# A hybrid attention, state-space and expert layer: the experts' weight pieces stored as contiguous blocks in the chip's memory

## The chip, the core and the metric

The kernel runs on one core of one Trainium2 chip, the other cores idle. The metric is the device time of one execution in microseconds; the median of the runs counts. Laying out the inputs with numpy on the host happens ahead of the execution and is no part of that time.

## The reference, cut to what matters

The layer is attention and a state-space branch, a product with `w_out`, a norm, and then a mixture of experts with a second norm. The change touches the mixture alone. Of 32 experts, each token (256 of them, 2048 features) is sent to two; an expert is a gated product of three matrices, gate and up of 2048 × 512 and down of 512 × 2048, all float32:

```python
def hierarchical_moe(h, ..., w_gate, w_up, w_down):
    ...
    def expert_block(args):
        tok, e = args
        xb = h[tok]
        return (jax.nn.silu(xb @ w_gate[e]) * (xb @ w_up[e])) @ w_down[e]
```

The three matrices of all experts are 32 × 3 × 4.19 MB = 403 MB, of 472 MB that the kernel moves in all. Every expert is computed, so all of them are loaded once.

## The kernel before, in words

**Front.** Up to about 430 us the kernel computes the projections, the two mixers, `w_out`, the first norm and the routing.

**The experts** come in 16 pairs (0 to 15), 64 token places for each expert of a pair. A pair is one pass of the loop behind line 1333: gather its tokens' features (`gather`, L1165), gate and up products (L1340: each weight piece is the moving operand, 512 columns, the two experts side by side in the two halves of the array's columns), silu times up (`hidden`, L1228 and L1229), a transpose (L1233), the down products in four column chunks (L1370), and the weighted sums back to token order (`weighted`, `combine`, L1192 to L1205). While one pair's down products run, the next pair's tokens are gathered. Pairs 2 to 7 also add the residual's rows (`res_rows`, L1090; `residual`, L1102 and L1107). The last pair works in half-sized pieces, so that less is left to do behind the last load.

**The weight pieces.** The list `items` (L974 to L982) holds the loads in the order of use: per pair eight gate, eight up and eight down pieces of 1 MB, alternating between the two experts; in the last pair sixteen of each at 0.5 MB. A gate or up piece is four of the sixteen feature tiles: feature p·16 + k lies on partition p, so the piece reads 8 KB in one stretch for each partition, and partitions lie 32 KB apart. A down piece is one of four column chunks: partition p holds rows 4p to 4p + 3, and of each row 512 columns, which are four stretches of 2 KB, 8 KB apart. In the last pair gate and up pieces read 4 KB per partition, and down pieces four stretches of 1 KB.

**What sets the order of the loads.** All of them are issued by SP, in the order of `items`. `ring_load` (L988) takes a free slot of SBUF (8 KB per partition; `RING`, L56, lists 21 of them) and issues the load; `ring_take` (L1014) hands the tile to the matmuls and puts the slot back on the list; `ring_fill` (L1021) issues as many further loads as there are free slots. A load waits on SP for the last reader of its slot and for earlier loads in flight, and every load behind it in SP's order waits with it. The two places that form a load's source are these:

```python
                nc.sync.dma_start(t, src[e].rearrange("(p f) d -> p f d", p=P)[:, :, lo:lo + w])
            else:
                nc.sync.dma_start(t, src[e].rearrange("(p k) f -> p (k f)", p=P)[:, q[0] * FE:(q[0] + q[1]) * FE])
```

**Behind the pairs** a loop takes tokens past an expert's first 64 in blocks of 128 (L1389 on; the number of blocks is read at run time), with loads of its own (L1423, L1434), and then comes the second norm and the store (L1443 to L1468).

Of the kernel before, what the change touches and what calls it, by code (L numbers as in the profile page):

```python
# [17 lines left out]
PSUM = bass.MemoryType.PSUM  # L18

P = 128  # L20
T = 256
D = 2048
# [10 lines left out]
NE = 32  # L33
# [4 lines left out]
# 8 KB slots of SBUF per partition, by use  # L38
# [21 lines left out]
def bcast_rows(ap, n=P):  # L60
    """A DRAM row vector, the same on n partitions."""
    return bass.AP(tensor=ap.tensor, offset=ap.offset, ap=[[0, n]] + [list(d) for d in ap.ap])
# [3 lines left out]
def block_kernel(ctx: ExitStack, tc: tile.TileContext, I: dict, out: bass.AP):  # L66
# [23 lines left out]
    # ---------------------------------------------------------------- first loads  # L90
# [9 lines left out]
    # ---------------------------------------------------------------- constants  # L100
# [108 lines left out]
    # ---------------------------------------------------------------- the dense products' weight pieces  # L209
    # a piece: four k-tiles of a column chunk, split into two parts of 12 significant bits each  # L210
# [41 lines left out]
    # ---------------------------------------------------------------- x transposed, in two parts  # L252
# [23 lines left out]
    # ---------------------------------------------------------------- parameter columns, rotary tables  # L276
# [14 lines left out]
    def rope_table(tab, pos, n, cols, name):  # L291
        """cos and sin of position * inv_freq: [n, cols, (cos, sin), 8]."""
        pf = fr.tile([n, cols, 1], F32, name=name + "_pf")
        dve.tensor_copy(pf[:, :, 0], pos)
        ang = wk.tile([n, cols, 2, 8], F32, name=name + "_ang", tag="qrt")
        for j in range(8):
            dve.tensor_scalar(ang[:, :, :, j], pf.to_broadcast([n, cols, 2]), float(INV_FREQ[j]), None, op0=OP.mult)
        k = wk.tile([n, cols, 2, 8], F32, name=name + "_k", tag="qrs")
        dve.tensor_scalar(k[:, :, 0], ang[:, :, 0], 1.0 / (2 * math.pi), 0.25, op0=OP.mult, op1=OP.add)
        dve.tensor_scalar(k[:, :, 1], ang[:, :, 1], 1.0 / (2 * math.pi), None, op0=OP.mult)  # L300
        dve.tensor_scalar(k, k, MAGIC, None, op0=OP.add)
        dve.tensor_scalar(k, k, -MAGIC, None, op0=OP.add)
        kf = k.rearrange("p a b c -> p (a b c)")
        af = ang.rearrange("p a b c -> p (a b c)")
        for c in (TWO_PI_1, TWO_PI_2, TWO_PI_3):
            dve.scalar_tensor_tensor(af, kf, -c, af, op0=OP.mult, op1=OP.add)
        dve.tensor_scalar(ang[:, :, 0], ang[:, :, 0], math.pi / 2, None, op0=OP.add)
        dve.tensor_scalar(ang, ang, 3.1415925, -3.1415925, op0=OP.min, op1=OP.max)
        act.activation(tab, ang, AF.Sin)

    def rope(dst, src, cos, sin, tmp):
        """dst[..., 0:16] = src[..., 0:16] rotated."""
        x1, x2 = src[..., 0:8], src[..., 8:16]
        dve.tensor_mul(tmp[..., 0:8], x2, sin)
        dve.tensor_mul(tmp[..., 8:16], x1, sin)
        dve.tensor_mul(dst[..., 0:8], x1, cos)
        dve.tensor_mul(dst[..., 8:16], x2, cos)
        dve.tensor_sub(dst[..., 0:8], dst[..., 0:8], tmp[..., 0:8])
        dve.tensor_add(dst[..., 8:16], dst[..., 8:16], tmp[..., 8:16])

    # ---------------------------------------------------------------- dense products
# [59 lines left out]
    # ---------------------------------------------------------------- what follows a chunk  # L381
# [96 lines left out]
    # ---------------------------------------------------------------- gates, time steps  # L478
# [4 lines left out]
    def gates_dt():  # L483
        gf = gates.rearrange("p a h c -> p (a h c)")
        act.activation(gf, gf, AF.Exp, scale=-1.0)
        dve.tensor_scalar(gf, gf, 1.0, None, op0=OP.add)
        dve.reciprocal(gf, gf)
        # softplus = max(x, 0) + ln(1 + exp(-|x|))
        dneg = fr.tile([P, 2, 16], F32, name="dneg")
        dve.tensor_scalar(dneg, dt, -1.0, None, op0=OP.mult)  # L490
        dve.tensor_tensor(dneg, dneg, dt, op=OP.min)
        act.activation(dneg, dneg, AF.Exp)
        act.activation(dneg, dneg, AF.Ln, bias=1.0)
        dve.tensor_scalar(dt, dt, 0.0, None, op0=OP.max)
        dve.tensor_add(dt, dt, dneg)
        act.activation(nega, nega, AF.Exp)
        dve.tensor_scalar(nega, nega, -1.0, None, op0=OP.mult)
        for a in range(2):
            dve.tensor_mul(dta[:, a], dt[:, a], nega)
# [17 lines left out]
    # ---------------------------------------------------------------- compressed keys and values  # L517
# [22 lines left out]
    def cmp_hidden():  # L540
        # four column tiles: (k or v, parity of the k-tile)
# [41 lines left out]
    def cmp_keys_t():  # L583
# [4 lines left out]
        # per group: high parts, low parts  # L588
# [18 lines left out]
    # ---------------------------------------------------------------- attention  # L607
# [24 lines left out]
    def cmp_scores(g):  # L632
        """Probabilities of the compressed branch times its gate: [token, (head, block)]."""
# [87 lines left out]
    # ---------------------------------------------------------------- state space branch (one chunk, no earlier state)  # L721
# [98 lines left out]
    # ---------------------------------------------------------------- router on the sums before the first norm  # L820
    # logits = rstd * (sums @ (g * W) - mean * colsum(g * W)) + (b @ W + bias)
# [42 lines left out]
    def router_t(c):  # L864
        """Logits transposed, [36, token], from two k-tiles in two column tiles at once."""
# [20 lines left out]
    # ---------------------------------------------------------------- the order of the work  # L886
# [80 lines left out]
    # ---------------------------------------------------------------- the experts' weight pieces, in the order of use  # L967
    wgate, wup, wdown = I["w_gate"][0], I["w_up"][0], I["w_down"][0]
# [3 lines left out]
    # k-tiles of a gate or up piece  # L972
    GU = [(k, 4) for k in range(0, KT, 4)], [(k, 2) for k in range(0, KT, 2)]
    items = []  # L974
    for pr in range(NE // 2):
        gu = [(nm, src, 2 * pr + u, q) for nm, src in (("g", wgate), ("u", wup)) for q in GU[pr == LASTP] for u in range(2)]
        dn = [("d", wdown, 2 * pr + u, (lo, w)) for c, lo, w in (DOWN_LAST if pr == LASTP else DOWN) for u in range(2)]
        # the last two loads before the first pair go where the sums before the norm lie
# [5 lines left out]
    def second(i):  # L984
        """The last pair's pieces are half as large, a slot for two; the other half of a slot that is open."""
        return items[i][2] == 2 * LASTP + 1

    def ring_load(n=1):  # L988
        for i in range(ring["next"], min(ring["next"] + n, len(items))):
# [15 lines left out]
            if nm == "d":  # L1005
                lo, w = q
                t = t.rearrange("p (f d) -> p f d", f=4)
                nc.sync.dma_start(t, src[e].rearrange("(p f) d -> p f d", p=P)[:, :, lo:lo + w])
            else:
                nc.sync.dma_start(t, src[e].rearrange("(p k) f -> p (k f)", p=P)[:, q[0] * FE:(q[0] + q[1]) * FE])  # L1010
# [39 lines left out]
    # ---------------------------------------------------------------- first norm, without its scale and shift  # L1050
# [22 lines left out]
    # feature d = 16 q + k goes to [k, q]  # L1073
# [11 lines left out]
    # the residual alpha * (normed * g + b): rows over the partitions  # L1085
# [10 lines left out]
    def residual(j, a):  # L1096
        """Column chunk j of the scaled rows (j < 4), or of the shift (j >= 4), into the sums."""
# [11 lines left out]
    # ---------------------------------------------------------------- routing  # L1109
# [3 lines left out]
    # the group of the largest logit, the first of equals  # L1113
# [12 lines left out]
    # its two best experts, the first of equals  # L1126
# [20 lines left out]
    # rank among the expert's tokens, from 1; 0 where the token is not the expert's  # L1147
# [3 lines left out]
    # ---------------------------------------------------------------- experts, in pairs, 64 tokens each  # L1151
# [36 lines left out]
    def weighted(py, wsl, i):  # L1188
        """The weighted outputs of a chunk, in two parts that one pass each carries."""
# [20 lines left out]
    def sums_first(lo, w):  # L1210
        """The sums so far, to which a chunk's outputs come in PSUM."""
# [13 lines left out]
    def hidden(pg, pu, xg):  # L1225
        """silu(gate) * up, transposed; both in the second half of a tile for gathered tokens."""
# [15 lines left out]
    def weights():  # L1242
        """Softmax over the two best, times the group's probability."""
# [19 lines left out]
    # tokens past an expert's first 64 go in blocks of 128: which block is whose  # L1263
# [32 lines left out]
    # scale and shift of the second norm, over the partitions  # L1296
    gb = {}

    def split_rows2():
        """The rows in two parts, on partitions 0 and 32 up, that one pass adds up exactly."""  # L1300
# [84 lines left out]
    # ---------------------------------------------------------------- tokens past an expert's first 64  # L1385
# [3 lines left out]
    with tc.For_i(0, nblk, 1) as b:  # L1389
# [29 lines left out]
        for src, pp in ((wgate, pg), (wup, pu)):  # L1419
            for q in range(4):  # L1420
                t = slot(OVER[n % 4], "w_o")
                n += 1
                nc.sync.dma_start(t, src[bass.ds(e, 1)].rearrange("o (p q k) f -> p (o q) (k f)", p=P, q=4)[:, q])  # L1423
# [7 lines left out]
        for c in range(4):  # L1431
            t = slot(OVER[n % 4], "w_o").rearrange("p (f d) -> p f d", f=4)
            n += 1
            nc.sync.dma_start(t, wdown[bass.ds(e, 1)].rearrange("o (p f) d -> p (o f) d", p=P)[:, :, c * 512:(c + 1) * 512])  # L1434
# [6 lines left out]
    # ---------------------------------------------------------------- second norm  # L1441
# [43 lines left out]

# [15 lines left out]
```

## Time and profile before

| | |
|---|---|
| median of 3 runs | 1416.79 us (1415.51 to 1418.05) |
| span of the profiled execution, first to last instruction | 1414.3 us |
| its own time | not listed apart; the median lies 2.5 us above the span |
| TensorE matmuls busy | 1326.1 us, 94% |
| VectorE, ScalarE, GpSimd busy | 515.3 us, 358.0 us, 159.1 us |
| moved by DMA | 472.12 MB in 157686 packets, mean 334 GB/s |
| loads of gate, up and down, 1 MB each | 120 of each; 18.0, 19.8 and 14.5 us from issue to landing (median) |
| mean granted clock of TensorE | 0.983 of 2.4 GHz |

Matmuls are pipelined and their ends are modelled, so that a busy TensorE isn't one at its peak. The DMA share of a window is the mean busy share of the core's 16 DMA engines; it can read a few per cent above 1, which is to be taken as always busy. A window's row gives the stretch, its length, busy time and count of instructions of PE (TensorE matmuls), PEld (its weight loads), DVE (VectorE), ACT (ScalarE) and POOL (GpSimd), then the granted clock, the DMA share and GB/s. A timeline's row gives the start, the time taken, the engine, the line and what it writes from what.

### The profile page before, as it was taken

To read this page: it belongs to the slowest core of one execution; us is meant where nothing else is said; L and a number is where in the kernel's file an instruction comes from. 1 tells how busy PE (TensorE), PEld (TensorE's weight loads), DVE (VectorE), ACT (ScalarE), POOL (GpSimd) and SP (SyncE) were. 2 spreads that over 40 slices of the span, in tenths; PEclk is the share of its full clock that TensorE was granted. 3 is DMA by queue.
4 is the path that set the end of the run, shared out by engine and by line. 5 is a ranking of instruction groups with operands and counts; after the bars stand their busy time and mean duration, and the time that the engine had idled before them with its cause. 6 is when DMAs were issued, how large, how long until landed. Compare 5 with 4: busy or idle time off the path is not lost. (4 is left out here: it accounts for less than half of the span.)

```text
span 1414.3 us, 18310 instructions
## 1 busy us (share of the span) xinstructions
PE 1326.1 (94%) x7381; PEld 765.6 (54%) x7381; DVE 515.3 (36%) x1095; ACT 358.0 (25%) x695; POOL 159.1 (11%) x87
## 2 busy tenths in 40 slices
PE   7998999999999999999999999999999998989994
PEld 6778899997784444434444343443444344343442
DVE  6757677568842323132131221312213021121216
ACT  4544566546423211111011110211101011010122
POOL 3432233334520000000000000000000000000001
PEclk9999999999999999999999999999999999999997
DMA  8852334436998999999999999999999999999993
GB/s 286 301 170 99 120 103 137 149 127 214 315 375 311 363 374 414 407 404 417 400 420 400 413 408 404 417 399 421 401 412 409 403 418 399 420 400 411 400 373 137
DMA packets 157686, 472.12 MB, mean 334 GB/s; under 512 B 17923, under 2 KB 32383, under 8 KB 126623
## 3 DMA queue, kind: packets, MB, share of 16 engines
q1 hardware_dynamic: 157008, 470.84, 86.4%
q8 instruction: 60, 0.98, 0.3%
q14 instruction: 28, 0.22, 0.0%
q0 software_dynamic: 288, 0.08, 0.0%
q10 hardware_dynamic: 302, 0.00, 0.0%
HBM read 468.79 MB, written 2.10 MB: 333 GB/s over the span
## 5 line engine op out<-in xcount | busy, mean ns | idle before, releaser
L1370 PE MATMUL p_dn<-wd,xg 128*64 128x512 f32 (+1 forms) x1088 | 244.6, 591 | 15.4 <-DVE work L1193 14.2
L1340 PE MATMUL p_up<-wu,xg 128*64 128x512 f32 x1024 | 229.1, 593 | 9.0 <-DMA wu<-in_w_up 9.0
L1340 PE MATMUL p_gate<-wg,xg 128*64 128x512 f32 x1024 | 226.0, 597 | 0.0
L243 POOL TENSOR_TENSOR w_lo<-raw,w_hi 128x1024 fp32r<-128x1024 f32 x52 | 141.6, 2727 | 252.1 <-ACT w_hi L242 239.0
L1340 PEld LDWEIGHTS p_up<-wu,xg 128*64 128x64 f32 x1024 | 76.3, 137 | 157.7 <-issue 134.3
L1229 DVE TENSOR_TENSOR xg<-xg,p_up 128x512 f32<-128x512 f32 x16 | 11.0, 688 | 409.0 <-ACT xg L1228 409.0
L1370 PEld LDWEIGHTS p_dn<-wd,xg 128*64 128x64 f32 x1088 | 74.8, 140 | 145.2 <-issue 109.3
L1340 PEld LDWEIGHTS p_gate<-wg,xg 128*64 128x64 f32 x1024 | 71.7, 137 | 143.7 <-issue 140.4
L1193 DVE SCALAR_TENSOR_TENSOR work<-p_dn,wsl,work 128x512 fp32r<-128x512 f32 (+1 forms) x68 | 48.9, 719 | 273.5 <-ACT work L1192 273.5
L1165 PEld LDWEIGHTS p_g<-S,hp 128*128 128x128 f32 x1024 | 120.8, 194 | 28.3 <-issue 26.0
L1165 PE MATMUL p_g<-S,hp 128*128 128x128 f32 x1024 | 127.2, 281 | 0.9 <-DVE cnt L1318 0.9
L1464 POOL TENSOR_TENSOR sum<-sum,row 128x512 f32<-128x512 f32 x4 | 6.7, 1692 | 995.7 <-DVE sum L1456 995.7
L242 ACT CAST w_hi<-raw 128x1024 fp32r<-128x1024 f32 (+1 forms) x112 | 108.5, 1020 | 31.9 <-PE p_acc L367 11.5
L1192 ACT ACTIVATE work<-p_dn,wsl 128x512 fp32r<-128x512 f32 (+1 forms) x68 | 45.2, 665 | 281.9 <-PE p_dn L1370 278.8
L345 PE MATMUL p_acc<-xh,w_hi 128*128 128x256 f32 x384 | 112.5, 293 | 0.0
L1228 ACT ACTIVATE xg<-p_gate 128x512 f32<-128x512 f32 x16 | 9.6, 597 | 406.6 <-PE p_up L1340 406.6
L347 PE MATMUL p_acc<-xl,w_hi 128*128 128x256 f32 x384 | 109.6, 285 | 0.0
L348 PE MATMUL p_acc<-xh,w_lo 128*128 128x256 f32 x384 | 109.6, 285 | 0.0
L243 DVE TENSOR_TENSOR w_lo<-raw,w_hi 128x1024 fp32r<-128x1024 f32 (+1 forms) x60 | 77.5, 1292 | 28.3 <-ACT w_hi L242 28.1
L1205 DVE TENSOR_TENSOR sum<-sum,p_co 128x512 f32<-128x512 f32 (+1 forms) x130 | 79.7, 650 | 9.4 <-PE p_co L1201 9.4
L1201 PE MATMUL p_co<-work,swT 128*128 128x512 f32 (+1 forms) x268 | 76.7, 408 | 0.0
L345 PEld LDWEIGHTS p_acc<-xh,w_hi 128*128 128x128 f32 x384 | 74.8, 195 | 0.7
(401 smaller groups left out, 1482.7 us busy)
## 6 DMA issues: line engine op xcount, KB each, us to landing
wg<-in_w_gate SPq DMA_DIRECT2D x120, 1024.0 KB, 18.0
wu<-in_w_up SPq DMA_DIRECT2D x120, 1024.0 KB, 19.8
wd<-in_w_down SPq DMA_DIRECT2D x120, 1024.0 KB, 14.5
raw<-in_w_in SPq DMA_DIRECT2D x36, 1024.0 KB, 5.0
raw<-in_w_out SPq DMA_DIRECT2D x16, 1024.0 KB, 5.2
wg<-in_w_gate SPq DMA_DIRECT2D x16, 512.0 KB, 10.8
wu<-in_w_up SPq DMA_DIRECT2D x16, 512.0 KB, 10.2
wd<-in_w_down SPq DMA_DIRECT2D x16, 512.0 KB, 8.9
```

What stands on the lines that cost most here:

```text
L242: act.copy(hi[:, ks, s], raw[:, ks])
L243: eng.tensor_tensor(lo[:, ks, s], raw[:, ks], f(hi[:, ks, s]), op=OP.subtract)
L345: pe.matmul(dst, hi[:, k, s], xk(xh, kt), start=(first and k == 0 and j % 2 == 0), stop=False, skip_group_check=True)
L347: pe.matmul(dst, hi[:, k, s], xk(xl, kt), start=False, stop=False, skip_group_check=True)
L348: pe.matmul(dst, lo[:, k, s], xk(xh, kt), start=False, stop=(last and k == 3), skip_group_check=True)
L1165: pe.matmul(at(k), hpm[a][:, 4 * c + k], S[:, a], start=(a == 0), stop=(a == 1))
L1192: act.activation(hi, py, AF.Copy, scale=wsl)
L1193: dve.scalar_tensor_tensor(lo, py, wsl, f(hi), op0=OP.mult, op1=OP.subtract)
L1201: pe.matmul(pc, swT[:, a * P:(a + 1) * P], part, start=(y == 0), stop=(y == 1))
L1205: dve.tensor_add(acc[a][:, s], acc[a][:, s], pc)
L1340: pe.matmul(pp[64 * u:64 * u + 64, :], xg[:, kk, 64 * u:64 * u + 64], tl[u][:, k], start=(kk == 0), stop=(kk == KT - 1), skip_group_check= ...
L1370: pe.matmul(py[64 * u:64 * u + 64, :], aT[:, q, 64 * u:64 * u + 64], tl[u][:, q], start=(q == 0), stop=(q == 3), skip_group_check=True)
```

## The change

The host stores the experts' weights in another order before the launch. `w_gate` and `w_up` become [expert, quarter, partition, 2048 elements], `w_down` [expert, column chunk, partition, 4 rows × 512 columns]; each 1 MB piece is then one contiguous block, 8 KB per partition. For the last pair's half chunks of down there is a further array, `w_down_last`, cut in eight, 4 KB per partition; the last pair's gate and up pieces read half of a partition's 8 KB, as they read 4 KB before. What lands in SBUF, and where, stays as it was, and so does all arithmetic. The loads of the loop over tokens past 64 follow the new order. Comments and docstrings go, too, so that line numbers behind L963 move by one to fourteen.

```diff
-    wgate, wup, wdown = I["w_gate"][0], I["w_up"][0], I["w_down"][0]
+    wgate, wup, wdown, wdown_last = I["w_gate"], I["w_up"], I["w_down"], I["w_down_last"]
...
             if nm == "d":
                 lo, w = q
+                nc.sync.dma_start(t, src[e, lo // 512] if w == 512 else wdown_last[e - 2 * LASTP, lo // w])
                 t = t.rearrange("p (f d) -> p f d", f=4)
-                nc.sync.dma_start(t, src[e].rearrange("(p f) d -> p f d", p=P)[:, :, lo:lo + w])
             else:
-                nc.sync.dma_start(t, src[e].rearrange("(p k) f -> p (k f)", p=P)[:, q[0] * FE:(q[0] + q[1]) * FE])
+                nc.sync.dma_start(t, src[e, q[0] // 4][:, q[0] % 4 * FE:(q[0] % 4 + q[1]) * FE])
                 t = t.rearrange("p (k f) -> p k f", f=FE)
...
-                nc.sync.dma_start(t, src[bass.ds(e, 1)].rearrange("o (p q k) f -> p (o q) (k f)", p=P, q=4)[:, q])
+                nc.sync.dma_start(t, src[bass.ds(e, 1), q].rearrange("o p x -> p (o x)"))
...
-            nc.sync.dma_start(t, wdown[bass.ds(e, 1)].rearrange("o (p f) d -> p (o f) d", p=P)[:, :, c * 512:(c + 1) * 512])
+            nc.sync.dma_start(t, wdown[bass.ds(e, 1), c].rearrange("o p x -> p (o x)"))
+            t = t.rearrange("p (f d) -> p f d", f=4)
...
+def _laid_out(inputs):
+
+    a = {name: np.ascontiguousarray(inputs[name]) for name in _INS}
+    for name in ("w_gate", "w_up"):
+        a[name] = np.ascontiguousarray(a[name][0].reshape(NE, P, 4, 4 * FE).transpose(0, 2, 1, 3))
+    down = a["w_down"][0].reshape(NE, P, 4, D)
+    cut = lambda v, n: np.ascontiguousarray(v.reshape(len(v), P, 4, n, D // n).transpose(0, 3, 1, 2, 4)).reshape(
+        len(v), n, P, -1)
+    a["w_down"], a["w_down_last"] = cut(down, 4), cut(down[-2:], 8)
+    return a
...
-    for name in _INS:
-        a = np.ascontiguousarray(inputs[name])
+    for name, a in _laid_out(inputs).items():
```

The order of the instructions is the same on every engine. On SP, at the change from the first pair's pieces to the second's, the kernel before issues these (`wg`, `wu` and `wd` are gate, up and down pieces; the sizes are the target's partitions and elements, as the source is cut):

```order
L1010 DMA wu<-in_w_up 128x2048 x5
L1008 DMA wd<-in_w_down 128x4x512 x5
L1010 DMA wu<-in_w_up 128x2048 x2
L1008 DMA wd<-in_w_down 128x4x512 x3
L1010 DMA wg<-in_w_gate 128x2048 x8
```

and the changed kernel, at the same place:

```order
L1011 DMA wu<-in_w_up 128x2048 x5
L1008 DMA wd<-in_w_down 128x2048 x5
L1011 DMA wu<-in_w_up 128x2048 x2
L1008 DMA wd<-in_w_down 128x2048 x3
L1011 DMA wg<-in_w_gate 128x2048 x8
```

Nothing moved; a down piece's four stretches of 512 elements became one of 2048. In the last pair, 128x4x256 became 128x1024 in the same way.

## Rows read from the trace of the kernel before

**Rows 1.** The page: engines, busy tenths in 40 slices, DMA packets.

```profile
PE 1326.1 (94%) x7381; PEld 765.6 (54%) x7381; DVE 515.3 (36%) x1095; ACT 358.0 (25%) x695; POOL 159.1 (11%) x87
...
PE   7998999999999999999999999999999998989994
...
DMA  8852334436998999999999999999999999999993
...
DMA packets 157686, 472.12 MB, mean 334 GB/s; under 512 B 17923, under 2 KB 32383, under 8 KB 126623
```

**Rows 2.** The windows, cut at each pair's first gate matmul.

```profile
core 0: us, PE busy (x) PEld busy (x) DVE busy (x) ACT busy (x) POOL busy (x), PEclk, DMA share, GB/s
...
554.97:615.61 60.64, 58.10 (x286) 25.19 (x285) 15.00 (x27) 7.42 (x18) 0.00 (x0) 0.97 1.02 408
615.61:674.56 58.95, 56.40 (x286) 24.78 (x285) 15.02 (x27) 7.42 (x18) 0.00 (x0) 1.00 1.03 409
...
913.76:971.50 57.74, 55.18 (x283) 24.57 (x282) 11.61 (x23) 7.42 (x18) 0.00 (x0) 1.00 1.03 408
971.50:1029.25 57.75, 55.20 (x283) 24.58 (x282) 11.62 (x23) 7.41 (x18) 0.00 (x0) 1.00 1.02 408
1029.25:1090.90 61.65, 57.95 (x283) 25.96 (x282) 11.62 (x23) 7.42 (x18) 0.00 (x0) 0.97 1.03 409
1090.90:1152.34 61.44, 57.96 (x284) 25.39 (x283) 11.63 (x23) 7.42 (x18) 0.00 (x0) 0.97 1.02 409
1152.34:1213.00 60.66, 56.50 (x284) 24.91 (x283) 11.62 (x23) 7.42 (x18) 0.00 (x0) 1.00 1.02 408
1213.00:1274.90 61.90, 56.63 (x284) 24.82 (x283) 11.62 (x23) 7.42 (x18) 0.00 (x0) 1.00 1.02 408
1274.90:1336.47 61.57, 56.48 (x283) 25.61 (x282) 12.89 (x26) 8.03 (x19) 0.00 (x0) 1.00 1.03 405
```

**Rows 3.** TensorE's waits, 1029 to 1337 us: sum, times, longest.

```profile
PE p_up L1340 <- DMA wu<-in_w_up: 9.0, 8, 1.4
```

**Rows 4.** The timeline of the last pair's end; landing of its down loads (us).

```profile
1380.01 1.96 PE L1370 MATMUL p_dn<-wd,xg 128*64 128x256 f32 x16
...
1382.58 2.41 PE L1370 MATMUL p_dn<-wd,xg 128*64 128x256 f32 x16
...
1385.59 2.35 PE L1370 MATMUL p_dn<-wd,xg 128*64 128x256 f32 x16
...
1388.53 0.65 PE L1370 MATMUL p_dn<-wd,xg 128*64 128x256 f32 x2
1389.67 1.94 PE L1370 MATMUL p_dn<-wd,xg 128*64 128x256 f32 x14 [0.50 <-SPq L1389]
...
1380.34 1.41 SPq L1008 DMA_DIRECT2D wd<-in_w_down  x1
...
DMA to landing us min/median/max: 8.9/8.9/8.9
```

**Rows 5.** The windows by piece: gate/up, down, last gate/up, last down, x.

```profile
528.00:548.00 20.00, 17.45 (x91) 8.23 (x91) 5.62 (x12) 4.63 (x11) 0.00 (x0) 1.00 1.01 420
560.00:580.00 20.00, 20.00 (x96) 6.75 (x94) 3.42 (x5) 0.00 (x0) 0.00 (x0) 1.00 1.05 387
1340.00:1356.00 16.00, 16.00 (x77) 5.79 (x73) 0.00 (x0) 1.65 (x5) 0.00 (x0) 1.00 1.03 410
1376.00:1384.00 8.00, 8.00 (x65) 4.97 (x62) 6.31 (x17) 1.43 (x3) 0.00 (x0) 1.00 1.10 348
318.00:324.00 6.00, 6.00 (x32) 4.47 (x31) 4.31 (x9) 2.73 (x3) 3.00 (x1) 1.00 1.04 425
```

**Rows 6.** The timeline of SP's DMA queue: first gate issues of pairs 2, 10, 15.

```profile
511.20 11.11 SPq L1010 DMA_DIRECT2D wg<-in_w_gate  x8
...
1004.13 11.76 SPq L1010 DMA_DIRECT2D wg<-in_w_gate  x8
...
1312.88 22.01 SPq L1010 DMA_DIRECT2D wg<-in_w_gate  x16
```

More of the change, by code (lines that the diff above doesn't have):

```diff
@@ L1431, in block_kernel @@
         for c in range(4):
-            t = slot(OVER[n % 4], "w_o").rearrange("p (f d) -> p f d", f=4)
+            t = slot(OVER[n % 4], "w_o")
             n += 1
-            nc.sync.dma_start(t, wdown[bass.ds(e, 1)].rearrange("o (p f) d -> p (o f) d", p=P)[:, :, c * 512:(c + 1) * 512])
+            nc.sync.dma_start(t, wdown[bass.ds(e, 1), c].rearrange("o p x -> p (o x)"))
+            t = t.rearrange("p (f d) -> p f d", f=4)
             py = bank("acc", "p_dn")
```

## The prediction

> **What bounds the kernel now.** The page comes first. TensorE shows as busy in 94% of the span, and so do the DMA engines: from the eleventh of the forty slices to the last but one both lines read 9 or 8 [rows 1]. Two resources that look full can't both be the bound of one stretch, so the next view is the windows, cut at the first gate matmul of each pair of experts [rows 2]. Call the pairs 0 to 15. Pairs 8 and 9 each take 57.75 us. Pairs 2 to 7 also carry the residual rows; they take 58.95 us, or 60.64 us where the granted clock fell. Those two differ by 1.7 us, and the longer one shows a mean clock of 0.97 in place of 1.00, a short stay on the lower of the two levels (1.2 instead of 2.4 GHz). Pairs 10 to 14 do the work of 8 and 9 and take 60.66 to 61.90 us.
>
> What they wait for stands in the waits of TensorE in that stretch: only the wait on the loads of the up weights is new, 9.0 us in 8 stalls [rows 3]. That row counts idle time alone. Around each stall the matmul stream also thins out, so I price the stalls by the lengths of the pairs: 61.65 + 61.44 + 60.66 + 61.90 + 61.57 = 307.2 us against 5 × 57.75 = 288.75 us, an excess of 18.5 us. Two of the five show the clock of 0.97, so 2 × 1.7 = 3.4 us is the clock's, and **15.1 us** the loads'.
>
> The last pair stalls too [rows 4]. Sixteen of its down matmuls should take 1.96 us, and three groups take 2.41 us, 2.35 us, and 3.08 us (0.65 us, a gap, then 1.94 us, ending at 1391.61 from 1388.53): together **2.0 us** too long. The last piece was issued at 1380.34 and landed 8.9 us later, at 1389.2, and the matmuls go on right behind it.
>
> Why do the loads fall behind only after pair 9? A pair's weights are 24 pieces of 1.049 MB, 25.17 MB. In windows that hold mainly pieces of one kind, the engines all busy, gate and up move at 420 GB/s and down at 387 [rows 5]. A pair therefore costs the DMA engines 16.78/0.420 + 8.39/0.387 = 39.95 + 21.7 = 61.6 us, more than TensorE needs. The ring hides that until its lead is eaten up: SP issued pair 2's first gate load at 511.20, 43.8 us before its use, and pair 10's at 1004.13, 25.1 us before [rows 6, 2]. At 25 us the stalls begin. The usable lead is **18.7 us**.
>
> **The change, part by part.**
>
> *Down pieces of pairs 0 to 14.* Each partition now reads 8 KB in one run, not four runs of 2 KB. Rates go with the run length: 348 GB/s for 1 KB (the last pair's down), 387 for 2 KB, 410 for 4 KB (the last pair's gate and up), 420 for 8 KB [rows 5]. A sixteenth of each, per engine, gives 47, 85, 160 and 312 ns per run: an estimate of some 10 ns per run beside 37 ps per byte. This is why I take 420 for the new down pieces: their form becomes that of the gate pieces. The ends are 387 (the run length isn't the cause) and 425 (the load of x into the sums, the one transfer of a whole contiguous megabyte, 318 to 324 us [rows 5]). The pair then costs 25.17/0.420 = 59.9 us, 1.7 us less.
>
> The Trainium skill has another price for short runs, in "DMA: Bandwidth & Descriptors", section "Why small descriptors are slow (HBM only)": about 3 extra cycles per packet on top of one per 32 bytes. By that, 2 KB against 8 KB would be only 3.5% apart, an estimate of 400 GB/s for the new down pieces; the rows here show 9% between the two lengths. What a rate part of the way would give is the first rival.
>
> *Gate and up pieces.* Their runs were 8 KB before, too; only the distance from partition to partition shrinks, from 32 to 8 KB. I take zero. Above it the bound is again 425, 1%; below it no row has an 8 KB run slower than 420, and what a loss would cost is the third rival.
>
> *Last pair.* Down goes from 1 KB to 4 KB runs, 348 to 410 GB/s: 24.1 to 20.5 us. Gate and up keep 4 KB runs.
>
> *Issues, engines, the overflow loop.* The order on SP and on each engine stays. The loop over tokens past 64 isn't entered in the trace (no row on its loads), so its edits cost nothing. What SP takes to issue isn't on the path: a pair's issues run 25 us and more ahead of their use, and were that cover gone, the stalls priced above would be what it costs. The layout is made on the host ahead of the launch.
>
> **The ledger.** Where the DMA engines need less than TensorE, the ring stays full and nothing more is won, since pieces wait for slots. Pairs 2 to 7 last 358.8 us (554.97 to 913.76), 59.8 each, against 59.9: the lead falls by 0.7 us. Pairs 8 to 14 fall by 7 × (59.9 − 57.75) = 15.1 us, or 11.7 with two clock drops. Of 18.7 us, 2.9 to 6.3 remain, so **no pair stalls**. Last pair: 1389.2 − 1312.88 = 76.3 us passed from its first issue to the last landing, 65.0 of them transfer (40.9 + 24.1), 11.3 backlog. Now 61.4 + 11.3 = 72.7 us. TensorE wants that piece 51.2 us after the pair's first matmul (1388.53 − 1336.47, less the two earlier stalls), so at least 25.1 + 2.9 + 51.2 = 79.2 us after the first issue. It is there 6 us early.
>
> What is late next is TensorE itself, with the lengths of pairs 8 and 9. The gain is 15.1 + 2.0 = **17.1 us**. The profiled span, 1414.3 us, becomes 1397.2; the median of the runs lies 2.5 us above the span, which gives **1399.7 us**.
>
> The clock is the unknown left: 1.7 us per drop. Drops in pairs 1 to 9 (three here) used to be swallowed by the later wait for loads; now each counts. None in the last five pairs gives 1396.3, five 1404.8.
>
> **The rivals.**
>
> 1. *Part of the way.* The new down pieces get halfway, 403 GB/s. The pair costs 39.95 + 20.8 = 60.8 us; the lead falls by 6 × 1.0 + 7 × 3.05 − 3.4 = 24 us, 5 more than there is: 1405 us. Against it: one price per run fits all four lengths. This is what the skill's 3 cycles would come to. Chance 0.08.
>
> 2. *Nothing.* The down pieces' lower rate isn't due to the runs, or the source isn't one run after all: 387 stays, the lead is eaten as before, 1416.8 us. Against it: 1 and 4 KB runs in the last pair lie apart in the same way, with other neighbours; of 157686 packets, all but 31,000 are under 8 KB [rows 1], which is what 240 gate and up pieces of 128 runs give, so such a tile does load in 8 KB runs. The Trainium skill ("DMA: Bandwidth & Descriptors", section "Where 436 GB/s comes from") says that the memory's share of about 358 GB/s binds such loads, by which run length wouldn't matter; the 420 GB/s of this trace disagrees. Chance 0.05.
>
> 3. *Slower.* A piece is now one contiguous megabyte, and the sixteen engines read close together. If that costs rate, it hits all 24 pieces. The point that decides is the mean of now, 25.17/61.6 = 409 GB/s. At 400 a pair costs 62.9 us, 1.3 more; 14 pairs bind one after the other from the ring's filling on, 18 us, less some 2 us won in the last pair: 1433 us. For it: no row shows a long stream of such pieces. Against it: the 425 GB/s of x. Chance 0.06.
>
> **How the numbers follow.** My forecast has a chance of 0.80, the rivals 0.08, 0.05 and 0.06; 0.01 is left over. The likeliest time is 1399.7 us. The forecast's own range is 1395 to 1405: up to five drops of the clock up, and down the none of them, with 1 us for the early pairs. I let the range go to 1406, which takes in rival 1 and leaves out rivals 2 and 3, with a tail below. About 0.2%, 2.8 us, is what a measurement of this kernel tells from no change: the three runs lie 2.5 us apart. Forecast and rival 1 are faster beyond that, 0.88; rival 2 is the same, with the leftover, 0.06; rival 3 slower, 0.06.
>
> **What would show it.** Right: the windows of the down pieces move 420 GB/s; pairs 10 to 14 take 57.75 us, or 59.45 with a clock below 1.00; the wait of the up matmuls on loads is gone; first issue to use stays above 25 us; packets fall by 52,224 (136 transfers, three runs in four gone), to about 105,000. Wrong: the down windows stay under 400, or gate and up fall below 420, or stalls remain in pairs 13 to 15 although the rates are right; then the ring's lead, not the rate, was misread.

## The result, and the profile after

The changed kernel takes 1398.8 us (median of 4 runs, 1397.74 to 1399.46) against 1417.4 us for the kernel before, measured beside it (4 runs, 1415.51 to 1418.23): a ratio of 0.9868, 95% interval 0.9854 to 0.9882. The forecast was 1399.7 us.

Two lines of the page after, and its packets, answer to [rows 1]. The DMA engines are still busy to the end, and yet no matmul waits for a load any more:

```profile
PE   7998999999999999999999999999999999999994
...
DMA  8943333446897899999999999999999999999991
...
DMA packets 105461, 472.12 MB, mean 338 GB/s; under 512 B 17922, under 2 KB 24190, under 8 KB 59038
```

52,225 packets are gone. The windows cut at each pair's first gate matmul, as in [rows 2]: pairs 2 and 3, then pairs 9 to 14. Columns as there.

```profile
core 0: us, PE busy (x) PEld busy (x) DVE busy (x) ACT busy (x) POOL busy (x), PEclk, DMA share, GB/s
556.82:617.47 60.65, 58.10 (x286) 25.18 (x285) 15.00 (x27) 7.42 (x18) 0.00 (x0) 0.97 1.01 420
617.47:676.42 58.95, 56.41 (x285) 24.78 (x284) 15.03 (x27) 7.42 (x18) 0.00 (x0) 1.00 1.01 421
...
973.37:1031.12 57.75, 55.19 (x283) 24.58 (x282) 11.62 (x23) 7.42 (x18) 0.00 (x0) 1.00 1.01 421
1031.12:1088.87 57.75, 55.20 (x284) 24.60 (x283) 11.62 (x23) 7.42 (x18) 0.00 (x0) 1.00 1.01 421
1088.87:1146.62 57.75, 55.19 (x283) 24.58 (x283) 11.62 (x23) 7.42 (x18) 0.00 (x0) 1.00 1.01 421
1146.62:1204.37 57.75, 55.20 (x284) 24.59 (x283) 11.63 (x23) 7.42 (x18) 0.00 (x0) 1.00 1.01 421
1204.37:1263.75 59.38, 56.82 (x283) 24.97 (x282) 11.61 (x23) 7.42 (x18) 0.00 (x0) 0.97 1.01 421
1263.75:1321.50 57.75, 55.19 (x283) 24.59 (x283) 12.90 (x26) 8.03 (x19) 0.00 (x0) 1.00 1.02 414
```

Pairs 10 to 14, formerly 60.66 to 61.90 us, are now at the 57.75 us of pair 9, save pair 13, whose clock of 0.97 costs it 1.6 us. Their DMA rate, 405 to 409 GB/s before, is 421 now, in pair 14 414. These are all waits of TensorE's matmuls from 440 to 1400 us (sum, times, longest); the wait on a load, which stood in [rows 3] with 9.0 us, is gone:

```profile
PE p_sw L1178 <- ACT xg L1235: 24.0, 15, 1.6
PE p_dn L1371 <- DVE work L1194: 14.3, 30, 0.5
PE p_ht L1234 <- DVE xg L1230: 1.5, 1, 1.5
PE p_dn L1371 <- ACT xg L1235: 0.7, 1, 0.7
PE p_co L1215 <- DVE sum L1206: 0.3, 1, 0.3
```

The timeline of the last pair's down groups answers to [rows 4]. Each takes 1.95 us, the last one too:

```profile
1367.59 1.95 PE L1371 MATMUL p_dn<-wd,xg 128*64 128x256 f32 x16
...
1370.13 1.95 PE L1371 MATMUL p_dn<-wd,xg 128*64 128x256 f32 x16
...
1372.68 1.95 PE L1371 MATMUL p_dn<-wd,xg 128*64 128x256 f32 x16
```

The windows by piece, as in [rows 5]: gate and up, then the stretch of the down pieces, then a stretch of half-sized pieces in the last pair, down among them:

```profile
528.00:548.00 20.00, 17.92 (x102) 9.50 (x101) 5.64 (x13) 4.08 (x11) 0.00 (x0) 1.00 1.01 420
560.00:580.00 20.00, 20.00 (x94) 6.56 (x92) 3.71 (x5) 0.00 (x0) 0.00 (x0) 1.00 1.01 422
...
1340.00:1356.00 16.00, 13.85 (x67) 5.36 (x67) 0.69 (x1) 4.88 (x11) 0.00 (x0) 1.00 1.03 409
```

And SP's timeline, with the first gate issues of pairs 2, 10 and 15, as in [rows 6]:

```profile
513.05 11.10 SPq L1011 DMA_DIRECT2D wg<-in_w_gate  x8
...
987.35 14.73 SPq L1011 DMA_DIRECT2D wg<-in_w_gate  x8
...
1284.19 27.99 SPq L1011 DMA_DIRECT2D wg<-in_w_gate  x16
```

From first issue to first use these pairs now have 43.8, 43.8 and 37.3 us; before they had 43.8, 25.1 and 23.6.

Where the time went can be added up between the two profiled executions. Pairs 10 to 14 together last 290.4 us (4 × 57.75 + 59.38) instead of 307.2: 16.8 us. The last pair, from its first gate matmul to the end of its last down matmul, lasts 53.1 us (1321.50 to 1374.63) instead of 55.1: 2.0 us. The first pair starts later by 1.8 us (434.19 instead of 432.42), a difference between executions and not the change's: in the twelve profiled executions of all kernels here it starts at 430.4 to 435.2 us, with no order by layout. 16.8 + 2.0 − 1.8 = 17.0 us, and the spans differ by 1414.3 − 1397.4 = 16.9.

### The profile page after: what moved, and what is told of

Its sections match the earlier page's. It is cut to its first block, busy times and chain, and to the rows that moved or that the text cites. A ratio compares the mean times of both kernels' runs of the same rounds, so it can differ in the third digit from the quotient of the medians.

```text
span 1397.4 us, 18310 instructions
## 1 busy us (share of the span) xinstructions
PE 1318.9 (94%) x7381; PEld 763.4 (55%) x7381; DVE 515.4 (37%) x1095; ACT 357.9 (26%) x695; POOL 159.2 (11%) x87
## 5 line engine op out<-in xcount | busy, mean ns | idle before, releaser
L1371 PE MATMUL p_dn<-wd,xg 128*64 128x512 f32 (+1 forms) x1088 | 241.3, 587 | 15.0 <-DVE work L1194 14.3
L1341 PE MATMUL p_up<-wu,xg 128*64 128x512 f32 x1024 | 222.9, 592 | 0.0
L1341 PEld LDWEIGHTS p_up<-wu,xg 128*64 128x64 f32 x1024 | 73.3, 137 | 145.6 <-issue 143.8
```

The lines of the kernel that those rows point to most:

```text
L1341: pe.matmul(pp[64 * u:64 * u + 64, :], xg[:, kk, 64 * u:64 * u + 64], tl[u][:, k], start=(kk == 0), stop=(kk == KT - 1), skip_group_check= ...
L1371: pe.matmul(py[64 * u:64 * u + 64, :], aT[:, q, 64 * u:64 * u + 64], tl[u][:, q], start=(q == 0), stop=(q == 3), skip_group_check=True)
```

## The experiments

Two theories stood against each other. **A**: what counts is how long the stretches are that one partition of a down piece reads; each stretch has a fixed price. **B**: what counts is that a piece is one contiguous block, so gate and up gain from it as well. Besides, it was open which of the last pair's edits matter, what bounds the kernel now, and how much room the loads still have.

**Gate and up alone.** Down as in the kernel before:

```diff
-                nc.sync.dma_start(t, src[e, lo // 512] if w == 512 else wdown_last[e - 2 * LASTP, lo // w])
                 t = t.rearrange("p (f d) -> p f d", f=4)
+                nc.sync.dma_start(t, src[e].rearrange("(p f) d -> p f d", p=P)[:, :, lo:lo + w])
```

> Gate and up pieces contiguous, down as in the kernel before. Theory A (the length of the down pieces' runs is what counts): no change against before, 1414 to 1420 us, gate and up windows at 420 GB/s, down windows at 387, pairs 10 to 14 at 60.7 to 61.9 us. Theory B (a piece that is one contiguous block loads faster): two thirds of the bytes gain, gate and up above 420 GB/s, at the 425 of x a pair costs 61.2 us instead of 61.6, so 1411 to 1413 us.

Measured: 1416.9 us, ratio to before 1.0002 (0.9993 to 1.0011). No change. The windows of gate and up (first) and of down (second) move what they moved before, although all gate and up pieces are contiguous now:

```profile
528.00:548.00 20.00, 17.92 (x100) 9.41 (x99) 5.44 (x12) 4.55 (x11) 0.00 (x0) 1.00 1.01 420
560.00:580.00 20.00, 20.00 (x92) 6.68 (x94) 3.71 (x5) 0.00 (x0) 0.00 (x0) 1.00 1.04 386
```

**Down alone.** Gate and up as in the kernel before:

```diff
-                nc.sync.dma_start(t, src[e, q[0] // 4][:, q[0] % 4 * FE:(q[0] % 4 + q[1]) * FE])
+                nc.sync.dma_start(t, src[e].rearrange("(p k) f -> p (k f)", p=P)[:, q[0] * FE:(q[0] + q[1]) * FE])
```

> Down pieces contiguous, gate and up as in the kernel before. Theory A: all of the gain is here, 1397 to 1401 us, a ratio of 0.987 to before. Theory B: a third to two thirds of the gain, 1404 to 1410 us.

Measured: 1398.4 us, ratio 0.9871 (0.9855 to 0.9888), which is the whole gain. The new layout of gate and up, two thirds of the bytes, does nothing.

**Long runs, but apart.** Down pieces read 8 KB per partition, and the partitions lie 32 KB apart, as they do in gate and up before; gate and up themselves are as in the kernel before:

```diff
-                nc.sync.dma_start(t, src[e, lo // 512] if w == 512 else wdown_last[e - 2 * LASTP, lo // w])
+                nc.sync.dma_start(t, src[e, :, lo // 512] if w == 512 else wdown_last[e - 2 * LASTP, :, lo // w])
...
-    cut = lambda v, n: np.ascontiguousarray(v.reshape(len(v), P, 4, n, D // n).transpose(0, 3, 1, 2, 4)).reshape(
-        len(v), n, P, -1)
+    cut = lambda v, n: np.ascontiguousarray(v.reshape(len(v), P, 4, n, D // n).transpose(0, 1, 3, 2, 4)).reshape(
+        len(v), P, n, -1)
```

> Down pieces with one run of 8 KB per partition (4 KB in the last pair), but partitions 32 KB apart, so that no piece is a contiguous block; gate and up as in the kernel before. Theory A: as with contiguous blocks, 1397 to 1401 us, 420 GB/s in the down windows. Theory B: as the kernel before, 1415 to 1419 us, 387 GB/s.

Measured: 1400.3 us, ratio 0.9884 (0.9868 to 0.9899). Not one piece is contiguous here, and the second window, the down pieces', still rises from 387 to 422:

```profile
528.00:548.00 20.00, 17.93 (x107) 10.13 (x108) 6.11 (x13) 4.33 (x11) 0.00 (x0) 1.00 1.01 421
560.00:580.00 20.00, 20.00 (x92) 6.45 (x90) 3.72 (x5) 0.00 (x0) 0.00 (x0) 1.00 1.01 422
```

The intervals of this run and of the changed kernel overlap. Theory B has fallen.

**The last pair as before.** Its down halves read stretches of 1 KB again; all else is the changed kernel:

```diff
-    a["w_down"], a["w_down_last"] = cut(down, 4), cut(down[-2:], 8)
+    a["w_down"], a["w_down_last"] = cut(down, 4), np.ascontiguousarray(down[-2:]).reshape(2, FE, D)
...
+                if w != 512:
+                    nc.sync.dma_start(t, wdown_last[e - 2 * LASTP].rearrange("(p f) d -> p f d", p=P)[:, :, lo:lo + w])
```

> The changed kernel, but the last pair's down halves read runs of 1 KB as before. If the last pair's shorter transfer is worth its 2.0 us (the term of the sum), 1400.8 us against 1398.8. If the lead that the earlier pairs keep covers it (the first issue of the last pair runs 37 us ahead of its use, against 25 where stalls begin; the runs cost 3.6 us more): no stall, 1397.5 to 1399.5 us.

Measured: 1398.5 us, ratio 0.9864 (0.9849 to 0.9879), as the changed kernel. The loads are slower, 342 GB/s in the window that gave 409 with 4 KB,

```profile
1340.00:1356.00 16.00, 13.85 (x66) 5.43 (x66) 0.69 (x1) 4.88 (x11) 0.00 (x0) 1.00 1.05 342
```

but they start early enough, so that no matmul waits. The separate array for the last pair earns nothing here.

**Stretches of 4 KB, and of 1 KB.** Each down piece of pairs 0 to 14 in two stretches per partition, then in eight (`r=8`):

```diff
-                nc.sync.dma_start(t, src[e, lo // 512] if w == 512 else wdown_last[e - 2 * LASTP, lo // w])
+                if w == 512:
+                    nc.sync.dma_start(t.rearrange("p (r x) -> p r x", r=2), src[e, lo // 512].rearrange("r p x -> p r x"))
+                else:
+                    nc.sync.dma_start(t, wdown_last[e - 2 * LASTP, lo // w])
...
+    a["w_down"] = np.ascontiguousarray(a["w_down"].reshape(NE, 4, P, 2, -1).transpose(0, 1, 3, 2, 4))
```

> The changed kernel with the down pieces (pairs 0 to 14) in two runs of 4 KB per partition. One price per run, some 10 ns: the down windows move 410 GB/s, a pair costs the DMA engines 60.4 us instead of 59.9; the spare lead of 12 us at the last pair covers that, so no stall and 1397.5 to 1400.5 us. If only runs of 8 KB escape a penalty: 387 GB/s and about 1414 us.

Measured: 1401.3 us, ratio 0.9881 (0.9861 to 0.9900), 0.8 us above the stated stretch. The rate is the one forecast; the window of the down pieces:

```profile
560.00:580.00 20.00, 20.00 (x94) 6.67 (x96) 3.69 (x5) 0.00 (x0) 0.00 (x0) 1.00 1.03 412
```

What I had wrong was the room. Pairs 13 and 14 of this run: the first is 0.3 us over the 57.75, the second takes 62.01 us, of which 1.7 us are the clock's, and TensorE stalls once on an up piece for 1.4 us.

```profile
1202.75:1260.80 58.05, 55.51 (x284) 25.48 (x283) 11.62 (x23) 7.40 (x18) 0.00 (x0) 1.00 1.02 416
1260.80:1322.81 62.01, 58.11 (x284) 25.18 (x283) 12.90 (x26) 8.02 (x19) 0.00 (x0) 0.97 1.02 412
```

Some 0.6 us more per pair (25.17 MB at 416 or 417 GB/s instead of 421) was enough to use the lead up at the end. The distance from first issue to first use in pair 15 overstates the room, 12 us. Counted from landing it is smaller: that first gate load lands 18.6 us ahead of its use in the kernel after and 10.9 us ahead in the stalled kernel before, 7.7 us apart.

> The changed kernel with the down pieces (pairs 0 to 14) in eight runs of 1 KB per partition. One price per run: 348 GB/s in the down windows, a pair costs 39.95 + 24.1 = 64.05 us, 2.45 more than in the kernel before, over some 13 pairs 32 us, less up to 3.6 us for the last pair's longer runs: 1441 to 1451 us. If the run length had little to do with it: below 1425 us.

Measured: 1446.8 us, ratio 1.0204 (1.0188 to 1.0220). The window in the middle of the down pieces, and the wait of TensorE on up pieces (sum, times, longest):

```profile
625.00:635.00 10.00, 10.00 (x50) 3.30 (x46) 0.27 (x1) 0.00 (x0) 0.00 (x0) 1.00 1.08 352
```

```profile
PE p_up L1344 <- DMA wu<-in_w_up: 31.8, 28, 1.7
```

Slower by 29 us in the same arithmetic, run backwards: 352 GB/s where 348 were expected, a stall in every pair from 7 on. With 1, 2, 4 and 8 KB the down windows now read 352, 387, 412 and 422 GB/s (387 in the kernel before, 386 with gate and up contiguous as in the others).

**Half of each down piece.** Is TensorE the bound now? Only half of a down piece is loaded, and the number of packets stays:

```diff
-                nc.sync.dma_start(t, src[e, lo // 512] if w == 512 else wdown_last[e - 2 * LASTP, lo // w])
+                if w == 512:
+                    nc.sync.dma_start(t[:, :1024], src[e, lo // 512][:, :1024])
...
-                    pe.matmul(py[64 * u:64 * u + 64, :], aT[:, q, 64 * u:64 * u + 64], tl[u][:, q], start=(q == 0),
+                    pe.matmul(py[64 * u:64 * u + 64, :], aT[:, q, 64 * u:64 * u + 64], tl[u][:, q if pr == LASTP else q % 2], start=(q == 0),
```

> The changed kernel, but only the first 4 KB per partition of each down piece is loaded (pairs 0 to 14), and its two row tiles are used twice: down products of rows 2 and 3 of each partition are left out and replaced. A sixth less is loaded. If TensorE is the bound now (theory A): no change, 1397.5 to 1400.5 us. If loads still hold it back: faster, up to 1390 us.

Measured: 1399.5 us, ratio 0.9874 (0.9859 to 0.9889): no change against the changed kernel with 63 MB less to move. Pairs 8, 11 and 13:

```profile
912.56:970.31 57.75, 55.19 (x283) 24.58 (x282) 11.62 (x23) 7.42 (x18) 0.00 (x0) 1.00 0.92 363
1085.81:1145.25 59.44, 56.90 (x284) 24.98 (x283) 11.63 (x23) 7.42 (x18) 0.00 (x0) 0.97 0.92 349
1202.99:1260.74 57.75, 55.19 (x283) 24.58 (x282) 11.62 (x23) 7.42 (x18) 0.00 (x0) 1.00 0.89 337
```

The DMA engines rest now and then, 0.89 to 0.92 instead of 1.01, and the pairs take the same 57.75 us, or 59.44 at the lower clock.

**A transpose moved out of a wait.** If TensorE is the bound, the wait that the waits of the kernel after show first, 24.0 us in 15 pieces of 1.60, should be worth its time. `p_ht` is the transpose of the hidden values, `p_sw` that of the one-hots (the matrix that says which token sits at which place of a pair). They share one bank of PSUM, the memory that TensorE writes to, the bank "o", so that `p_sw` waits until ScalarE has emptied it. A bank of the gathers' pair is free by then:

```diff
         S = SEL.pop(pr)
-        pt = bank("o", "p_sw")
+        pt = bank("t", "p_sw")
```

> The changed kernel, with the one-hots' transpose (p_sw) in the pair of PSUM banks of the gathers instead of in the one bank that it shares with the transpose of the hidden values. It need not wait 1.60 us for ScalarE to empty that bank; its 0.95 us of work fill the gap instead, 0.95 us in each of 15 pairs, 14 us, and the granted clock may fall less often behind the gap (1.7 us each, four times now). If TensorE is the bound now, faster by 9 to 14 us, 1385 to 1390 us: the spare lead, some 12 us, is the most that the loads allow. If loads bound it already: 1397.5 to 1400 us.

Measured: 1389.7 us, ratio 0.9808 (0.9791 to 0.9824), 9.1 us under the changed kernel's median (8.5 us by the two ratios to the kernel before) and **the fastest that computes everything**. The timeline shows `p_sw` right behind `p_ht`; what is left of the gap, 1.04 us, waits for the hidden values themselves:

```profile
988.43 0.64 PE L1234 MATMUL p_ht<-ident,xg 128*128 128x128 f32 x4
988.90 0.38 PE L1178 MATMUL p_sw<-ident,S 128*128 128x128 f32 x2
989.12 0.51 PE L1180 MATMUL p_sw<-wt,S 128*128 128x2 f32 x4
990.66 1.51 PE L1371 MATMUL p_dn<-wd,xg 128*64 128x512 f32 x6 [1.04 <-ACT xg L1235]
```

But pairs 11 and 12 (after pair 9, in the first row) don't get the 57.04 us. They take what the loads need, 25.17 MB at 421 GB/s, 59.8 us:

```profile
957.13:1014.17 57.04, 55.05 (x284) 24.57 (x283) 11.62 (x23) 7.30 (x18) 0.00 (x0) 1.00 1.01 421
...
1071.29:1130.93 59.64, 56.34 (x283) 24.76 (x282) 11.62 (x23) 7.29 (x18) 0.00 (x0) 1.00 1.01 421
1130.93:1190.60 59.67, 56.35 (x284) 24.76 (x283) 11.63 (x23) 7.30 (x18) 0.00 (x0) 1.00 1.01 421
```

**Both.** The moved transpose, and half of each down piece:

> Both the transpose in the gathers' banks and the down pieces loaded by half (the same part of the down products left out as before: rows 2 and 3 of each partition in pairs 0 to 14). The run with the transpose moved stalled on loads in pairs 10 to 14 (59.6 us each against 57.03 in pairs 8 and 9). If the loads are what bounds it there, every pair takes 57.03 us (58.24 with residual rows), no clock drop, and the time is some 11 to 13 us below that run's 1389.7: 1376 to 1379 us. If something else has come up in those pairs: 1386 to 1391 us.

Measured: 1379.3 us, ratio 0.9740 (0.9728 to 0.9753), 0.3 us above the stated stretch. (The pairs that stall in the run before are 11 to 14, not 10 to 14; the last of them takes 61.21 us.) Pairs 13 and 14 now take 57.04 and 57.03 us:

```profile
1187.54:1244.58 57.04, 55.05 (x284) 24.57 (x283) 11.63 (x23) 7.29 (x18) 0.00 (x0) 1.00 0.91 351
1244.58:1301.61 57.03, 55.05 (x284) 24.55 (x283) 12.89 (x26) 7.89 (x19) 0.00 (x0) 1.00 0.97 367
```

So in the run before it was the loads that took some 10 us back.

**The moved transpose in the kernel before.** The same line, on the old layout:

> The kernel before, with the transpose moved in the same way. If the loads bind its end (theory A), TensorE's shorter pairs only use up the ring's lead sooner: 1414 to 1418 us, no change. If TensorE's time counted there as it does in the changed kernel: 1405 to 1409 us.

Measured: 1416.3 us, ratio 1.0001 (0.9991 to 1.0010). Pairs 9, 11 and 13, and the wait on the up pieces, which grew from 9.0 to 21.9 us:

```profile
964.31:1027.17 62.86, 56.78 (x283) 24.85 (x282) 11.62 (x23) 7.30 (x18) 0.00 (x0) 1.00 1.02 409
1088.66:1150.04 61.38, 56.55 (x284) 24.89 (x283) 11.62 (x23) 7.29 (x18) 0.00 (x0) 1.00 1.02 409
1212.57:1274.43 61.86, 56.55 (x283) 25.42 (x282) 11.62 (x23) 7.31 (x18) 0.00 (x0) 1.00 1.02 409
```

```profile
PE p_up L1340 <- DMA wu<-in_w_up: 21.9, 20, 1.4
```

What TensorE saves, it waits for later. The same edit is worth some 9 us behind the change and nothing ahead of it.

## Why the prediction was right, point by point

*What bounds the kernel.* Shown from both sides. Ahead of the change, time that TensorE saves comes back as waits on up pieces, 12.9 us more of them, and the kernel is no faster (the last run). Behind it, a sixth of an expert pair's bytes can be left out without effect (the run with half pieces).

*The down pieces' rate.* 420 GB/s forecast, 422 measured in the window. The estimate behind it, a fixed price per stretch beside a price per byte, held when the down pieces themselves took the two other lengths, whose rates had been read in the last pair's half-sized pieces alone: 412 GB/s against 410, 352 against 348. The kept traces also time each DMA packet, one for each stretch. In the down windows shown a packet takes a median of 51, 88, 164 and 312 ns for 1, 2, 4 and 8 KB (the runs with 1 and 4 KB, the kernels before and after): an estimate of 14 ns beside 36 ps per byte (the DMA shares there, 1.01 to 1.08, say that packets overlap a little, so that the rates show some 10 ns). The price is thus in the DMA engines' own time for a stretch, and not only in SP's time for issuing it. The 3 extra cycles per packet of the Trainium skill ("DMA: Bandwidth & Descriptors", section "Why small descriptors are slow (HBM only)"), by which the down pieces would have come to an estimated 400 GB/s, are too few for what was measured here. Rival 1 has fallen with it.

*Gate and up at zero.* Right: 1.0002 (0.9993 to 1.0011). Rival 3, slower by contiguity, falls with the same run, and rival 2 with the change itself.

*The ledger.* That no pair stalls came out as said. Its size, 18.7 us of usable lead and 2.9 to 6.3 us left, can be checked in two runs, by the stretch from pair 2 to the last pair that no load has lengthened: pairs 2 to 5 with 1 KB stretches, pairs 2 to 10 with the moved transpose:

```profile
556.08:795.27 239.19, 229.00 (x1137) 99.93 (x1137) 55.84 (x101) 29.68 (x69) 0.00 (x0) 0.99 1.05 391
```

```profile
550.63:1071.29 520.66, 502.73 (x2552) 222.77 (x2551) 116.55 (x215) 65.71 (x154) 0.00 (x0) 1.00 1.01 421
```

At these rates four pairs need 257.5 us and nine 538.0: the ring had covered an estimated 18.3 and 17.4 us. In the kernel after, pairs 2 to 14 last 764.7 us and their loads need 777.2 at 421 GB/s, 12.5 us more, so that an estimated 5 to 6 us were left. For the run with 4 KB stretches I took a larger room, 12 us, by the distance from issue to use, and that was the mistake. The ledger would have foretold its stall: 13 pairs at 60.4 us need 785 us, TensorE 763 (three clock drops, no stall), a shortage of 22 us against 18.7.

*The sum.* 15.1 us of stalls and 2.0 us in the last pair: both are gone in the trace. One clock drop fewer than assumed in pairs 10 to 14 (one, not two) gave 1.7 us more, and the later start of the first pair took 1.8 us. Neither could be known ahead; that they cancel is luck, worth some 1.8 us. The last pair's 2.0 us come from the earlier pairs' loads, not from its own longer stretches, as the run with its old down halves shows; I had put that edit's shorter transfer (24.1 to 20.5 us) into the ledger of the last pair as if it might be needed, and it isn't.

*From span to time.* I added 2.5 us. The runs of the kernel after lie 1.75 us above their spans (1399.15 over 1397.4 in the profiled one). So do listed runs of the kernel before (1416.92 over 1415.2): the 2.5 us had set one execution's span against the median of others. The 0.75 us between is the larger part of the 0.9 us by which the forecast lies above the median.

## What to carry to other kernels

Before an edit for TensorE, look at when its waits on loads begin. A deep ring of buffers hides a shortage of a few per cent for many rounds (here 61.6 us of loads a pair behind 57.75 to 60.65 us of TensorE's time, until pair 10), and after that every round takes the loads' time. The busy shares of the whole span don't show this; windows cut at each round do. Where the loads are the bound, count the stretches that one partition reads, not the size of the transfer: with down in 2 KB stretches, a third of the bytes, the whole stage ran at 409 GB/s instead of 421. And a layout that frees the loads also makes TensorE's idle time worth removing: the two together gave 28.2 us (1389.7 us against 1417.9 measured beside it), and the second without the first gave nothing.

## What had not been expected of the hardware

SP's own time for issuing a down piece fell, too, from a median of 1816 ns to 328 ns (minimum, median and maximum below, first the kernel before, then after). An issue of 512 stretches thus held SP for two thirds of the time that the piece takes to move (1.049 MB at 387 GB/s, 2.7 us), one of 128 for an eighth of it (2.5 us at 422). In the runs with 4 KB and 1 KB, 256 and 1024 stretches, the medians are 420 and 2872 ns.

```profile
L1008 SPq DMA_DIRECT2D wd<-in_w_down x136: 539/1816/9210, 407.9 to 1380.3; - x136
```

```profile
L1008 SPq DMA_DIRECT2D wd<-in_w_down x120: 327/328/882, 409.6 to 1281.7; - x120
```

No run separates what this is worth by itself; in the late pairs of the kernel before the DMA engines were always busy (a share of 1.02 or more), so there it can't have cost anything.

And the granted clock fell, at a cost of some 1.7 us each time, behind TensorE's idle 1.60 us: five pairs of the kernel before (2, 4, 6, 10 and 11) and four of the kernel after (2, 4, 6 and 13) show it behind that gap, while the other pairs up to 14 have the same gap and keep the clock behind it. Pair 2 of the kernel after, the gap in the first window and the lower clock in the second:

```profile
588.00:592.00 4.00, 2.40 (x23) 2.21 (x21) 1.10 (x4) 1.99 (x5) 0.00 (x0) 1.00 1.01 420
592.00:596.00 4.00, 4.00 (x15) 1.45 (x17) 0.00 (x0) 0.58 (x3) 0.00 (x0) 0.68 1.02 426
```

In the three profiled executions with the gap cut to 1.04 us no pair from 1 to 14 shows it, and the mean granted clock is 0.988 to 0.990 instead of 0.983. But in two of them (the moved transpose in the changed kernel and in the kernel before) the clock falls once in the last pair, after an idle 1.5 us of another wait and close to a second of 0.7 us, so the moved transpose doesn't end the falls for good. What besides the gap decides is open.
